# A down projection rearranged: 32 of its 44 feature tiles as seven block products with 512 moving columns

## The chip, the core and the metric

The kernel runs on one core of a Trainium2 chip. The metric is device time in microseconds of one execution. A core has TensorE (PE in the profile, its weight loads as PEld), VectorE (DVE), ScalarE (ACT), GpSimd (POOL) and SyncE (SP). Transfers are issued from SP's queue (hardware descriptors) and from POOL's queue (POOL writes the descriptors, so each issue shows as a busy POOL instruction).

## What is computed

One layer of an encoder for 512 tokens of 2048 features in float32: a norm, one projection to queries, keys and values, three kinds of attention, an output projection with a residual, then the part that matters here:

```python
h = rmsnorm(x, ffn_norm[l])
g = causal_dwconv(jnp.einsum('bsd,df->bsf', h, w_gate[l]), conv_w[l], conv_b[l])
u = jnp.einsum('bsd,df->bsf', h, w_up[l])
x = x + jnp.einsum('bsf,fd->bsd', jax.nn.silu(g) * u, w_down[l])
return rmsnorm(x, final_norm)
```

`w_down` is 5632 x 2048, so the last product takes 44 tiles of 128 gated features to 16 tiles of 128 outputs, for 512 tokens.

## The kernel before

Every product of float32 operands is made of three products of rounded parts: `split` (L57 to L59) writes the rounded high part on ScalarE (L58) and the rest on VectorE (L59), and `mm3` (L61 to L64) multiplies low by high, high by low and high by high into one PSUM bank. So each weight tile must pass ScalarE and VectorE before TensorE can use it. The pool of split weights, `wspl`, has three buffers of 1024 columns: a split can be made only when TensorE has finished with the part three places back.

The program has these stages, in order: attention with its projections (to about 710 us), the output projection (to 851 us), four gate and up tiles computed plainly and then 40 by `strassen` (to 1757 us), and the down projection with the last norm (to the end). TensorE's order is that of the code (`manual_schedule` on PE). The other engines' orders are set by the scheduler of the framework, which places an instruction by its estimated costs among what is ready.

`strassen(f)` computes gate and up of one feature tile as seven products of 256 tokens (Winograd's form). Its tiles come from two rings: `z`, into which POOL adds a second weight block while it loads (L804, an accumulating transfer), and five buffers `a` of pool `r4`. The gated tile is stored on POOL's queue into `a_dram` in the layout [128, 44, 512].

The down projection, `down` (after L920), takes the gated features in 11 chunks of 4 tiles. `gated(c)` loads one chunk from `a_dram` on SP's queue (`araw`) and splits it; `load_unit` loads 1 MB of weights for four output tiles into `wraw` (two buffers of 1 MB) and splits it in halves. Per output tile 12 matmuls run with the weights stationary and 512 tokens moving into one bank `dn`, and VectorE adds the bank to the residual `x2` (L938), which stays in SBUF for the whole stage in eight buffers of `big`. The residual is loaded on POOL's queue (L979) when TensorE has finished with the operands of the last gate tile. The last chunk is computed for 256 tokens at a time, so that the last norm of the first half runs beside the matmuls of the second.

Chunk by chunk this is 10 x 192 matmuls of 512 columns and 2 x 192 of 256 columns.

Of the kernel before, what the change touches and what calls it, by code (L numbers as in the profile page):

```python
# [15 lines left out]
P = 128  # L16
S = 512
# [6 lines left out]
NCH = NFT // CH  # L24
NEG = -3.0e38
# [16 lines left out]
def trunk(ctx, tc, xT, wqkv, wo, wo15, wgu, wd, par, lam4, rel, out):  # L42
# [14 lines left out]
    def split(hi, lo, src):  # L57
        act.copy(out=hi, in_=src)  # L58
        dve.tensor_tensor(out=lo, in0=src, in1=hi.bitcast(F32), op=ALU.subtract)  # L59
# [48 lines left out]
    a_dram = dram.tile([P, NFT, S], F32, name="a_dram")  # L108
# [123 lines left out]
    with ExitStack() as actx:  # L232
# [166 lines left out]
        def finish(o, summer, n, eps, gain, slot):  # L399

            sq = tmp.tile([P, S], F32, tag="t2", name="osq")
            act.activation(sq, o, AF.Square)
            sh = tmp.tile([P, S], F32R, tag="t2", name="osh")
            sl = tmp.tile([P, S], F32R, tag="t2", name="osl")
            split(sh, sl, sq)
            yield 7
            bank = att_bank("ossq")
            pe.matmul(bank, summer, sl, start=True, stop=False)
            pe.matmul(bank, summer, sh, start=False, stop=True)
            rs = rsqrt(None, bank, n, eps, tmp, "o")  # L410

            def last():
                split(y1[0][slot], y1[1][slot], o)

            dve.scalar_tensor_tensor(out=o, in0=o, scalar=gain, in1=rs, op0=ALU.mult, op1=ALU.mult)
            if slot >= KT - 2:
                pending.append(last)
            else:
                pool.dma_start(y_dram[:, slot, :], o)
# [277 lines left out]
    with ExitStack() as actx:  # L697
        fp = actx.enter_context(tc.tile_pool(name="fp", bufs=2))
        r4 = actx.enter_context(tc.tile_pool(name="r4", bufs=5))
# [24 lines left out]
        def new_g():  # L724
            g = fp.tile([P, 2 + 2 * S], F32, tag="g", name="g")
            pool.memset(g[:, 0:2], 0.0)
            return g, g[:, 2 + S : 2 + 2 * S]

        def plain(f):
# [12 lines left out]
            dve.tensor_tensor(out=u, in0=bu, in1=rs2, op=ALU.mult)  # L742
            dve.tensor_tensor(out=u, in0=u, in1=cv, op=ALU.mult)
            pool.dma_start(a_dram[:, f, :], u)
# [42 lines left out]
        def strassen(f, first=False):  # L787
# [18 lines left out]
            def later():  # L806
                a12, a22 = block("a12"), block("a22")
                sync.dma_start(a12, wgu[f, 0][:, half[1]])
                sync.dma_start(a22, wgu[f, 1][:, half[1]])
                return a12, a22  # L810

            def halves(src):
                wh = wspl.tile([P, 1024], F32R, tag="wh", name="wh")
                wl = wspl.tile([P, 1024], F32R, tag="wl", name="wl")
                split(wh, wl, src)
                return wh, wl
# [5 lines left out]
            lo, hi = slice(0, HS), slice(HS, S)  # L822
            U = fp.tile([P, HS], F32, tag="U", name="U", bufs=2)
# [26 lines left out]
            if first:  # L850
# [14 lines left out]
            else:  # L865
# [10 lines left out]
            w2 = halves(a12)  # L876
            add(a12, s2)
            product(w2, second, 1, bank1[:, lo], False, True)
            act.copy(out=g[:, 2 : 2 + HS], in_=bank1[:, lo])
            product(halves(a12), second, 2, bank2[:, lo], False, False)  # L880
            product(halves(a22), sums_, 3, bank2[:, hi], False, True)
            dve.tensor_tensor(
                out=g[:, 2 + HS : 2 + HS + S].rearrange("p (a b) -> p a b", b=HS),
                in0=bank2.rearrange("p (a b) -> p a b", b=HS),
                in1=U.unsqueeze(1).to_broadcast([P, 2, HS]),
                op=ALU.add,
            )
            cv, silu = convolved(f, g)
            dve.scalar_tensor_tensor(out=u, in0=u, scalar=-1.0, in1=cv, op0=ALU.mult, op1=ALU.mult)
            pool.dma_start(a_dram[:, f, :], u)  # L890
            return silu
# [6 lines left out]
        second = []  # L898
        for f in range(NPLAIN, NFT):
            silu = strassen(f, f == NPLAIN)  # L900


    with ExitStack() as actx:
        fp = actx.enter_context(tc.tile_pool(name="fp", bufs=2))
        x2 = None

        def gated(c):

            raw = wraw.tile([P, CH, S], F32, tag="raw", name="araw")
            sync.dma_start(raw, a_dram[:, c * CH : (c + 1) * CH, :])  # L910
            ah, al = [], []
            for i in range(CH // 2):
                j = (c % 2) * 2 + i
                h, l = [big.tile([P, 2, S], F32R, tag=f"b{x}{j}", name=f"a{x}") for x in "hl"]
# [5 lines left out]
        ssum3 = h2p.tile([P, S], F32, tag="ssum", name="ssum3")  # L920

        def down(units, a, t=slice(0, S), after=None, between=None):
            w = t.stop - t.start
            for g, halves in enumerate(units):
                for mm in range(4):
# [12 lines left out]
                    dve.tensor_tensor(out=x2[m][:, t], in0=bank, in1=x2[m][:, t], op=ALU.add)  # L938
                    if after is not None:
                        after(m, t)  # L940
                if between is not None:
                    next(between)

        def squares(m, t):
            sq = fp.tile([P, S], F32, tag="g", name="sq3")
# [6 lines left out]

        def last_norm(t, queues):
# [4 lines left out]
            rsqrt(rs3[:, t], ssq, D, NORM_EPS, fp, "n3", 3)  # L958
# [15 lines left out]
        a = gated(0)  # L974
        x2 = []
        for j in range(4, 8):
            for x in "hl":
                t = big.tile([P, 2, S], F32, tag=f"b{x}{j}", name="x2")
                pool.dma_start(t, x_dram[:, len(x2) : len(x2) + 2, :])  # L979
                x2 += [t[:, n, :] for n in range(2)]  # L980
# [5 lines left out]
        with tc.issue_after(silu):  # L986
            act.preload_act_table_set("natural_log_exp_and_others")
        t0, t1 = slice(0, S // 2), slice(S // 2, S)

        kept = [  # L990
            [h2p.tile([P, 1024], F32R, tag=f"h2{x}{i}", name=f"k{x}{i}") for x in "hl"] for i in range(8)
        ]
        kept = [kept[2 * g : 2 * g + 2] for g in range(4)]
        down((load_unit(wd[NCH - 1, g], kept[g]) for g in range(4)), a, t0, squares)
        down(kept, a, t1, squares, last_norm(t0, (sync,)))
# [71 lines left out]
```

## Time and profile before

| | |
|---|---|
| median of 3 runs | 2254.25 us (2253.73 to 2255.53) |
| the profiled execution, its own time | 2253.81 us |
| its span, first to last instruction | 2252.1 us |
| TensorE busy | 2209.6 us (98%), 14012 matmuls |
| VectorE busy | 1511.4 us (67%) |
| ScalarE busy | 992.8 us (44%) |
| POOL busy | 264.8 us (12%) |
| read from HBM, written to it | 305.65 MB, 27.79 MB |

How to read it: busy time is the union of an engine's instructions. A matmul's duration is its latency; matmuls overlap, and what one costs is the distance between the starts of two in a row. A group of instructions shows its line, engine, operation, the names of what it writes and reads, its shape and count, then its busy time, the mean duration of one, and the idle time of the engine just before. `SPq` and `POOLq` are the queues on which a transfer was issued; the number behind it is the median time from issue to landing.

### The profile page before, as it was taken

The page shows a single profiled execution, that of the slowest core. Times are in us where ns is not written, and L with a number is a line of the kernel's source. Part 1 is how long each engine was busy: PE and PEld are TensorE (multiplying, and loading weights), DVE is VectorE, ACT ScalarE, POOL GpSimd, SP SyncE. Part 2 cuts the span into 40 slices and gives each one's busy share as a digit, 9 for nine tenths or more (in the row PEclk, how much of TensorE's full clock was granted, in tenths as well). Part 3 has the DMA queues.
Part 4 walks back from the last instruction along what each step waited for, and adds up shares of the span by engine and source line. Part 5 has one row for each costly group of instructions (what it writes and reads, how often), then busy time and mean ns, then how long its engine had stood idle before and what let it go on. Part 6 is the DMA issues. An engine that isn't in the chain of part 4 may idle for free.

```text
span 2252.1 us, 34744 instructions
## 1 busy us (share of the span) xinstructions
PE 2209.6 (98%) x14012; PEld 2010.3 (89%) x14012; DVE 1511.4 (67%) x2169; ACT 992.8 (44%) x1482; POOL 264.8 (12%) x509
## 2 busy tenths in 40 slices
PE   8999999999999999999999999999999999999997
PEld 7888898788888888799999999999999888888887
DVE  6766667787677547777777777777777655555565
ACT  5555455566565323444444444444444322222232
POOL 0100001212112221011101111011110000000003
PEclk9999999999999999999999999999999999999999
DMA  5222222122234445867777777778775533333332
GB/s 196 99 80 85 99 80 90 64 87 72 97 126 158 169 137 205 272 182 204 193 197 186 204 200 198 190 189 206 198 196 154 210 113 112 131 118 125 131 131 76
DMA packets 79729, 335.69 MB, mean 149 GB/s; under 512 B 9424, under 2 KB 14288, under 8 KB 63184
## 3 DMA queue, kind: packets, MB, share of 16 engines
q1 hardware_dynamic: 56896, 257.32, 34.4%
q0 software_dynamic: 21376, 74.99, 14.4%
q8 instruction: 110, 1.80, 0.3%
q10 hardware_dynamic: 1296, 1.17, 0.2%
q14 instruction: 51, 0.42, 0.1%
HBM read 305.65 MB, written 27.79 MB: 148 GB/s over the span
## 4 chain that ended last, share of the span: by engine, by line
PE 90%; DVE 4%; ACT 2%; issue 1%; DMA 1%; POOL 1%; SPq 0%; POOLq 0%; DVEq 0%; ACTq 0%
PE c L64 36%; PE dn L64 21%; PE wo L64 8%; PE v L64 7%; PE q L64 6%; PE k L64 6%; PE tr L379 1%; PE g L64 1%; PE pv L64 1%; PE sc L349 1%; PE sc L348 1%; DVE l L530 1%; POOL z L500 1%; DVE wl L59 1%; PE u L64 0%
## 5 line engine op out<-in xcount | busy, mean ns | idle before, releaser
L58 ACT CAST wh<-raw 128x1024 fp32r<-128x1024 f32 (+1 forms) x227 | 236.1, 1041 | 502.1 <-PE dn L64 299.0
L59 DVE TENSOR_TENSOR wl<-a,wh 128x1024 fp32r<-128x1024 f32 x199 | 243.5, 1224 | 190.3 <-ACT wh L58 190.2
L64 PE MATMUL c<-bl,wh 128*128 128x256 f32 x1280 | 363.4, 284 | 3.8 <-ACT wh L58 3.8
L64 PE MATMUL c<-bh,wl 128*128 128x256 f32 x1280 | 363.3, 284 | 1.5 <-DVE wl L59 1.5
L64 PE MATMUL c<-bh,wh 128*128 128x256 f32 x1280 | 363.2, 284 | 0.0
L59 DVE TENSOR_TENSOR wl<-raw,wh 128x1024 fp32r<-128x1024 f32 (+1 forms) x227 | 274.4, 1210 | 96.3 <-ACT wh L58 95.7
L58 ACT CAST wh<-a 128x1024 fp32r<-128x1024 f32 x199 | 208.8, 1049 | 242.8 <-DVE a L819 205.0
L64 PE MATMUL c<-h2l,wh 128*128 128x256 f32 x960 | 271.8, 283 | 0.9 <-DVE U L844 0.9
L64 PE MATMUL c<-h2h,wh 128*128 128x256 f32 x960 | 271.7, 283 | 0.0
L64 PE MATMUL c<-h2h,wl 128*128 128x256 f32 x960 | 271.7, 283 | 0.0
L64 PEld LDWEIGHTS c<-bl,wh 128*128 128x128 f32 x1280 | 246.8, 193 | 4.0 <-ACT wh L58 4.0
L64 PE MATMUL dn<-al,wh 128*128 128x512 f32 x640 | 249.2, 389 | 0.7 <-DVE al L59 0.7
L938 DVE TENSOR_TENSOR x<-dn,x 128x512 f32<-128x512 f32 (+1 forms) x192 | 124.0, 646 | 187.1 <-PE dn L64 183.6
L64 PE MATMUL dn<-ah,wl 128*128 128x512 f32 x640 | 249.0, 389 | 0.0
L64 PE MATMUL dn<-ah,wh 128*128 128x512 f32 x640 | 249.0, 389 | 0.0
L64 PEld LDWEIGHTS c<-bh,wl 128*128 128x128 f32 x1280 | 246.7, 193 | 1.8 <-DVE wl L59 1.8
L64 PEld LDWEIGHTS c<-bh,wh 128*128 128x128 f32 x1280 | 246.7, 193 | 0.0
L64 PEld LDWEIGHTS c<-h2l,wh 128*128 128x128 f32 x960 | 184.3, 192 | 1.1 <-DVE U L844 1.1
L64 PEld LDWEIGHTS c<-h2h,wl 128*128 128x128 f32 x960 | 184.3, 192 | 0.0
L64 PEld LDWEIGHTS c<-h2h,wh 128*128 128x128 f32 x960 | 184.3, 192 | 0.0
L64 PE MATMUL v<-wl,hh 128*128 128x256 f32 x512 | 147.9, 289 | 10.1 <-DVE wl L59 9.2
L64 PE MATMUL v<-wh,hl 128*128 128x256 f32 x512 | 145.8, 285 | 0.4 <-DVE hl L161 0.4
(242 smaller groups left out, 4690.9 us busy)
## 6 DMA issues: line engine op xcount, KB each, us to landing
a<-in_wgu SPq DMA_DIRECT2D x121, 512.0 KB, 4.7
raw<-in_wqkv SPq DMA_DIRECT2D x46, 1024.0 KB, 4.8
raw<-in_wd SPq DMA_DIRECT2D x44, 1024.0 KB, 4.8
z<-in_wgu SPq DMA_DIRECT2D x80, 512.0 KB, 5.7
z<-in_wgu POOLq DMA_DIRECT2D x78, 512.0 KB, 9.8
raw<-in_wo SPq DMA_DIRECT2D x16, 1024.0 KB, 4.8
a_dram<-g POOLq DMA_DIRECT2D x44, 256.0 KB, 6.0
araw<-a_dram SPq DMA_DIRECT2D x11, 1024.0 KB, 4.9
```

The lines of the kernel that those rows point to most:

```text
L58: act.copy(out=hi, in_=src)
L59: dve.tensor_tensor(out=lo, in0=src, in1=hi.bitcast(F32), op=ALU.subtract)
L64: pe.matmul(o, l[x], r[y], start=start and i == 0, stop=stop and i == 2, skip_group_check=on)
L348: pe.matmul(bank[:, kt], q[c][:, qt], k[c][:, kt], start=True, stop=False)
L349: pe.matmul(bank[:, kt], q[c][:, qt], kh[c][:, kt], start=False, stop=True)
L379: pe.transpose(out=bank[:, (i - j) * P : (i - j + 1) * P], in_=w[:, o : o + P], identity=ident)
L500: pool.affine_select(out=t[:, o : o + P], in_=t[:, o : o + P], pattern=[[-1, P]], compare_op=ALU.is_gt, fill=fill, base=0, channel_multipl ...
L530: dve.tensor_tensor_scan(back, back, back, 0.0, ALU.add, ALU.max)
L938: dve.tensor_tensor(out=x2[m][:, t], in0=bank, in1=x2[m][:, t], op=ALU.add)
```

## The change

Chunks 0 to 7 (feature tiles 0 to 31) are no longer computed by `down`. They are computed four chunks at a time as a two by two block product, seven products instead of eight, with the gated features stationary and 512 columns of weights moving. The outputs are then tokens by features, are stored, and at the end are turned on TensorE and added to the residual. Chunks 8 to 10 stay in `down`. In parts:

- **Stores.** `store` puts tiles 0 to 31 into `ab_dram`, by halves of 256 tokens. For tiles 4 to 7, 12 to 15, 20 to 23 and 28 to 31, `tile_before` loads the tile stored four places earlier (two loads of 128 KB on SP), and `token_sums` makes the four sums of token halves on VectorE (four 128x256 operations) and stores them in `t_dram` (two stores of 256 KB on POOL). It writes into `g` and `cv`, which the tile has finished with.
- **Weights' sums for the first unit.** Beside attention, POOL copies four weight units of 1 MB from DRAM to DRAM (after the outputs of heads 0 to 3) and adds others to them by accumulating transfers (after heads 4 to 7).
- **The last gate tile** (`last=True`) runs its products in another order, those on `second` first, with separate banks, so that the buffers of `second` come free four products before its end.
- **`Seven`.** Four units: two groups of four chunks, times two pairs of 512 output columns. A unit has 28 steps (seven products, two blocks, two halves). A step splits 1024 columns of weights (L1127 on ScalarE, L1129 on VectorE) and issues 12 matmuls of 512 columns (two feature slices, two token tiles, three each). VectorE forms the weights' sums in place (`prepare`, `prepare_6`; the first unit finds half of its sums formed). The weights go through four buffers of 1 MB (`wraw` and a new pool `rw`). The gated operands, 14 per group of chunks, are loaded on POOL's queue through two buffers `fe` (the first four into freed buffers) and split by the table FIRST or NEXT at given steps. `sums` adds the products up out of PSUM and stores them on POOL into `c_dram`. This part has its orders on all engines from the code.
- **`turned`.** After a group of matmuls of chunks 8 and 9, two 1 MB tiles of `c_dram` are loaded on SP, added on VectorE (128x2048), turned by 16 transposes into four banks, and added to or taken from `x2`.
- The residual is loaded during the last unit; the load of ScalarE's tables moves from the end of the down projection to its beginning.

Counted over the program: 1536 matmuls of `dn` with 512 columns go; 1344 of the same shape into the seven products' banks `r`, and 64 transposes of 128x128, come.

```diff
+NSEV = 32
+    ab_dram = dram.tile([P, 2, NSEV, S // 2], F32, name="ab_dram")
+    t_dram = dram.tile([P, 4, NSEV // 2, S // 2], F32, name="t_dram")
+    a_dram = dram.tile([P, NFT - NSEV, S], F32, name="a_dram")
+    s_dram = [dram.tile([P, 2048], F32, name=f"s_dram{i}") for i in range(4)]
+    c_dram = [dram.tile([P, NB, D], F32, name=f"c_dram{i}") for i in range(NSEV // 16)]
...
+                if slot < 8:
+                    i = slot % 4
+                    b, w = divmod(i, 2)
+                    with tc.issue_after(stored):
+                        if slot < 4:
+                            pool.dma_start(s_dram[i], wd[2 * b, 0] if w else wd[2 * b + 1, 1])
+                        else:
+                            pool.dma_start(s_dram[i], wd[2 * b, 1], accum_op=ALU.add, max_dma_last_dim=8192)
...
+            dve.tensor_tensor(out=t1, in0=b11, in1=b12, op=ALU.subtract)
+            dve.tensor_tensor(out=t3, in0=b22, in1=b12, op=ALU.subtract)
+            for dst, x, y in ((t2, b22, t1), (t4, t2, b21)):
+                dve.scalar_tensor_tensor(out=dst, in0=x, scalar=-1.0, in1=y, op0=ALU.mult, op1=ALU.subtract)
+            for n, t in ((0, t12), (2, t34)):
+                pool.dma_start(t_dram[:, n : n + 2, f // 8 * 4 + f % 4, :], t.rearrange("p (a b) -> p a b", b=HS))
...
+            def parts(self, between):
+                src = self.src
+                wh = wspl.tile([P, 1024], F32R, tag="wh", name="wh")
+                wl = wspl.tile([P, 1024], F32R, tag="wl", name="wl")
+                hv, lv = [w.rearrange("p (i m c) -> p m i c", i=2, m=4) for w in (wh, wl)]
+                act.copy(out=hv, in_=src)
+                between()
+                dve.tensor_tensor(out=lv, in0=src, in1=hv.bitcast(F32), op=ALU.subtract)
+                self.ws = wh, wl
+            def multiply(self, k):
...
+                for i in range(2):
+                    o, w = (2 * h + i) * HS, slice(i * S, (i + 1) * S)
+                    for t in range(2):
+                        q = slice(o + t * P, o + (t + 1) * P)
+                        mm3(self.banks[r][t], (f[0][:, q], f[1][:, q]), (self.ws[0][:, w], self.ws[1][:, w]),
...
+            def sums(self, k):
...
+                elif k == 26:
+                    e = self.out_tile()
+                    for t in range(2):
+                        act.copy(out=e[:, t, :], in_=r["1"][t])
+                    self.put(e, 0, 0)
+                elif k == 28:
+                    e = self.out_tile()
+                    for t in range(2):
+                        add(e[:, t, :], r["5"][t], self.U[:, t, :])
+                    self.put(e, 0, 1)
...
+                for mm in range(4):
+                    x = x2[4 * g + mm]
+                    bank = acc_bank("ct")
+                    for t in range(NB):
+                        pe.transpose(
+                            out=bank[:, t * P : (t + 1) * P], in_=cs[0][:, t, mm * P : (mm + 1) * P], identity=ident
+                        )
+                    dve.tensor_tensor(out=x, in0=x, in1=bank, op=ALU.subtract if g % 2 else ALU.add)
...
-        a = gated(0)
...
-        for c in range(NCH - 1):
-            down((load_unit(wd[c, g]) for g in range(4)), a)
-            a = gated(c + 1)
+        rest = turned()
+        a = gated(c0, 14)
+        for c in range(c0, NCH - 1):
+            down((load_unit(wd[c, g]) for g in range(4)), a, plus, between=rest)
+            a = gated(c + 1, 8 if c == c0 else 14)
```

Two places in the order of instructions are spoken of below. The first is VectorE in the reduction. Before, in a chunk of `down` (`x2` the residual, `dn` a bank, `wl` and `al` the low parts of weights and features):

```order
L938 TENSOR_TENSOR x2_18096<-dn_18224,x2_18096 128x512
L59 TENSOR_TENSOR wl_18307<-raw_18304,wh_18306 128x1024
L938 TENSOR_TENSOR x2_18098<-dn_18248,x2_18098 128x512
L59 TENSOR_TENSOR al_18373<-araw_18370,ah_18372 128x1024
L59 TENSOR_TENSOR al_18377<-araw_18370,ah_18376 128x1024
L938 TENSOR_TENSOR x2_18098<-dn_18262,x2_18098 128x512
```

Now, at the opening of the second unit (`c`, `U` sums out of the banks `r5`, `r7`; `raw<-raw` and `sh`, `sl` the sums of weights):

```order
L1068 TENSOR_TENSOR c_18870<-r5_18323,U_18537 128x512
L1068 TENSOR_TENSOR c_18870<-r5_18324,U_18537 128x512
L1068 TENSOR_TENSOR raw_18823<-raw_18821,raw_18823 128x4x256
L1129 TENSOR_TENSOR wl_18875<-raw_18819,wh_18874 128x4x2x128
L1068 TENSOR_TENSOR raw_18823<-raw_18821,raw_18823 128x4x256
L1129 TENSOR_TENSOR wl_18892<-raw_18823,wh_18891 128x4x2x128
L1068 TENSOR_TENSOR U_18537<-r7_18365,U_18537 128x512
L1068 TENSOR_TENSOR U_18537<-r7_18366,U_18537 128x512
L1068 TENSOR_TENSOR raw_18821<-raw_18821,raw_18819 128x4x256
L1129 TENSOR_TENSOR wl_18914<-raw_18823,wh_18913 128x4x2x128
L1068 TENSOR_TENSOR sh_18918<-raw_18823,raw_18819 128x1024
L1068 TENSOR_TENSOR raw_18821<-raw_18821,raw_18819 128x4x256
```

Between two splits of weights there now stand sums of weights and sums out of PSUM, where before one or two residual additions stood. The second place is POOL's queue where the last gate tile meets the reduction. Before:

```order
L890 DMA a_dram_82<-g_17618 128x512
L979 DMA x2_18092<-x_dram_81 128x1024
L979 DMA x2_18090<-x_dram_81 128x1024
L979 DMA x2_18094<-x_dram_81 128x1024
L979 DMA x2_18096<-x_dram_81 128x1024
L979 DMA x2_18098<-x_dram_81 128x1024
L890 DMA a_dram_82<-g_17846 128x512
```

Now (`fh`, `fl` and `f` are the first gated operands):

```order
L752 DMA a_dram_84<-g_17765 128x512
L1047 DMA fh_18238<-ab_dram_82 128x1024
L1051 DMA fl_18239<-t_dram_83 128x1024
L1051 DMA fh_18240<-t_dram_83 128x1024
L1051 DMA fl_18241<-t_dram_83 128x1024
L1047 DMA f_18252<-ab_dram_82 128x1024
L1051 DMA f_18254<-t_dram_83 128x1024
L752 DMA a_dram_84<-g_17993 128x512
```

The residual's eight loads have gone from here to the last unit, and six loads of gated operands, 512 KB each, stand in their place.

More of the change, by code (lines that the diff above doesn't have):

```diff
@@ L918, in gated, with down @@
             return ah, al
-        ssum3 = h2p.tile([P, S], F32, tag="ssum", name="ssum3")
-        def down(units, a, t=slice(0, S), after=None, between=None):
+        def down(units, a, add, t=slice(0, S), between=None):
             w = t.stop - t.start
@@ L937, in down @@
                         )
-                    dve.tensor_tensor(out=x2[m][:, t], in0=bank, in1=x2[m][:, t], op=ALU.add)
-                    if after is not None:
-                        after(m, t)
+                    add(m, t, bank)
                 if between is not None:
-                    next(between)
-        def squares(m, t):
-            sq = fp.tile([P, S], F32, tag="g", name="sq3")
+                    next(between, None)
+        ORDER = [(n, b) for b in range(2) for n in (1, 5, 7, 6)] + [(n, b) for b in range(2) for n in (2, 3, 4)]
@@ new lines, in feature_parts, with weights, add @@
+        def feature_parts(i, src):
+            p = pair(10 + i if i < 6 else i - 6, name="f")
+            split(*p, src)
+            return p
+        raws = [0]
+        def weights(src):
+            raws[0] += 1
+            raw = (rw, wraw)[raws[0] % 2].tile([P, 2048], F32, tag="raw", name="raw")
+            sync.dma_start(raw, src)
+            return [raw.rearrange("p (m i c) -> p m i c", m=4, i=4)[:, :, 2 * h : 2 * h + 2, :] for h in range(2)]
+        def add(dst, x, y):
+            dve.tensor_tensor(out=dst, in0=x, in1=y, op=ALU.add)
```

311 lines of the change are left out of this document (263 added, 48 removed).

## The prediction

> **What bounds the kernel now.** I read the page first: busy shares, the granted clock by slices, the chain.
>
> ```profile
> span 2252.1 us, 34744 instructions
> PE 2209.6 (98%) x14012; PEld 2010.3 (89%) x14012; DVE 1511.4 (67%) x2169; ACT 992.8 (44%) x1482; POOL 264.8 (12%) x509
> ...
> PEclk9999999999999999999999999999999999999999
> ...
> PE 90%; DVE 4%; ACT 2%; issue 1%; DMA 1%; POOL 1%; SPq 0%; POOLq 0%; DVEq 0%; ACTq 0%
> ```
>
> TensorE is busy nearly all the time at full clock and carries 90% of the chain. Next I read the chain in order of time, for the stages that the change touches.
>
> ```profile
> 959.16 792.27 PE c L64 x6600
> 1756.68 462.93 PE dn L64 x2154
> 2220.05 15.84 PE dn L64 x132
> ```
>
> From 959 us to 2236 us the chain is matmuls alone: first gate and up (`c`), then the down projection (`dn`), with no other engine between. What an instruction of TensorE less is worth there is its full distance to the next one. Third, the busy time by stretches, and TensorE's waits from 951 us to 2220 us.
>
> ```profile
> core 0: us, PE busy (x) PEld busy (x) DVE busy (x) ACT busy (x) POOL busy (x), PEclk, DMA share, GB/s
> ...
> 959.00:1757.00 798.00, 797.10 (x6631) 796.28 (x6632) 582.13 (x634) 365.90 (x436) 95.12 (x157) 1.00 0.73 191
> 1757.00:2220.00 463.00, 463.00 (x2157) 388.33 (x2156) 247.42 (x291) 120.01 (x127) 14.67 (x21) 1.00 0.36 129
> 2220.00:2252.10 32.10, 18.01 (x147) 17.40 (x145) 22.73 (x53) 7.80 (x19) 8.47 (x12) 0.84 0.40 132
> ```
> ```profile
> engine line waited for: us in total, times, longest us
> PE c L64 <- DVE U L844: 0.9, 1, 0.9
> PE dn L64 <- DVE al L59: 0.7, 1, 0.7
> ```
>
> In the down projection TensorE has work at every moment, while VectorE is busy 247 of 463 us and the transfers fill 36%. There is room beside TensorE, and that is where the change puts its additions; whether they fit is the question.
>
> **What goes and comes on TensorE.** The price of a matmul of 512 columns is read where nothing else runs, in the stretch of `dn` alone; that of a transpose from the timeline of TensorE in attention, where five stand in a row.
>
> ```profile
> 1800.00:2000.00 200.00, 200.00 (x884) 165.61 (x883) 50.47 (x73) 1.00 0.33 116
> ```
> ```profile
> 400.06 0.71 PE L379 MATMUL tr<-ident,z 128*128 128x128 f32 x5
> ```
> ```profile
> L64 PE MATMUL dn<-al,wh 128*128 128x512 f32 x640 | 249.2, 389 | 0.7 <-DVE al L59 0.7
> ...
> L379 PE MATMUL tr<-ident,w 128*128 128x128 f32 x160 | 27.9, 272 | 0.0
> ```
>
> 884 matmuls in 200 us are 0.2262 us each; the 389 ns of a group's mean is latency, of which 163 ns overlap. 1536 of them go and 1344 of the same shape and type come: 192 x 0.2262 = 43.4 us less. Five transposes in 0.71 us, the last with its latency of 0.27, start (0.71 - 0.27) / 4 = 0.11 us apart: 64 of them cost 7.0 us more. Net on TensorE: -36.4 us. That the new matmuls hold a feature slice and stream weights changes neither shape nor type, so I leave their price; if it differed by 1 ns, it would be 1.3 us.
>
> The Trainium skill (TensorE: Matmul & The Clock Gate, Part 4: PE-mode transpose) gives about 275 ns for a 128x128 transpose in a kernel's context, and speaks so far against the change: 64 would be 17.6 us and the net -25.8 us. This case's row has the same 272 ns, but as latency; the starts lie 0.11 us apart, and the row decides.
>
> **Step time and its feeding.** A step of a unit is 12 matmuls, 12 x 0.2262 = 2.71 us; a unit of 28 steps is 76.0 us. Beside it VectorE has to do far more than `down` asked of it. Its prices:
>
> ```profile
> L59 DVE TENSOR_TENSOR wl<-raw,wh 128x1024 fp32r<-128x1024 f32 x223 | 272.7, 1224 | 95.4 <-ACT wh L58 94.9
> ...
> L938 DVE TENSOR_TENSOR x<-dn,x 128x512 f32<-128x512 f32 x160 | 110.6, 691 | 169.0 <-PE dn L64 165.6 <-DMA x<-x_dram 3.5
> ...
> L819 DVE TENSOR_TENSOR a<-a,z 128x1024 f32<-128x1024 f32 x40 | 49.0, 1225 | 1.4
> ...
> L844 DVE TENSOR_TENSOR U<-c,U 128x256 f32<-128x256 f32 x40 | 17.0, 425 | 13.8 <-ACT U L843 13.8
> ```
>
> In the second unit: 28 splits, 16 sums of weights and 7 splits of features, 51 x 1.225 = 62.5 us, and ten sums out of PSUM, 6.9 us: 69.4 of 76.0 us. The first unit has 8 sums fewer and 6 features more (67 us), the third equals the second, the fourth has no features (61 us). So VectorE fits on average, at 91% in the worst, but not evenly: what counts is how far a split may come late. ScalarE, 1.05 us per split, has 43 us and fits.
>
> ```profile
> 1403.02 1.05 ACT L58 CAST wh<-a 128x1024 fp32r<-128x1024 f32 x1 [0.81 <-PE c L64]
> ```
> ```profile
> 1404.18 1.22 DVE L59 TENSOR_TENSOR wl<-a,wh 128x1024 fp32r<-128x1024 f32 x1
> ```
>
> From the moment TensorE frees a buffer to the end of the split into it are 2.4 us (1403.02 to 1405.40). With three buffers the split is wanted two steps, 5.4 us, after that: a lead of 3.0 us. The worst place is the opening of each unit after the first, whose order stands above: from the sums out of `r5` to the split of the sixth step VectorE has 11 operations of 1.225 and four of 0.69 us, 16.2 us, against five steps of 13.6 us. The 2.6 us too much eat the lead of 3.0. The sums there also wait: those of `c` for the store of the previous `c` (one buffer), whose price is bounded by the nearest rows of POOL's queue:
>
> ```profile
> a<-in_wgu SPq DMA_DIRECT2D x121, 512.0 KB, 4.7
> raw<-in_wd SPq DMA_DIRECT2D x44, 1024.0 KB, 4.8
> ...
> z<-in_wgu POOLq DMA_DIRECT2D x78, 512.0 KB, 9.8
> ...
> b_dram<-b POOLq DMA_DIRECT2D x8, 512.0 KB, 4.6
> x<-x_dram POOLq DMA_DIRECT2D x8, 512.0 KB, 9.9
> xin<-in_xT SPq DMA_DIRECT2D x7, 512.0 KB, 10.1
> ```
>
> ScalarE fills that `c` after step 23; with 2.4 us of ScalarE and 4.6 us for a plain 512 KB store it has landed 7.5 us after that step's end, about when VectorE arrives (two steps and 2.4 us, 7.8 us). With 9.8 us, an accumulating load's, it would hold VectorE, with all splits queued behind, some 4 us in each unit: 16 us. I take 1 us per opening and 2 us for step 17 and the feature splits of the first unit, 5 us; bounds 0 and 16.
>
> **Entering the units.** POOL's first feature load waits for the last product on `second`, four products of 24 matmuls (24 x 792.27 / 6600 = 2.9 us) before the end, 11.5 us. Four loads of 512 KB then run at once with three of 1 MB on SP, which wait for the last split into `r4`'s ring, about 6 us before the end. At the 218 GB/s of the `raw<-in_wd` row the first features land after 5 us and are split before the end; the second weight unit, wanted 5.4 us after it, lands about 2 us after the end and still has two splits to pass, behind the tail of the last gate tile (two convolution steps, four sums, a product) on VectorE. I take 3 us; bounds 0 and 8 (if the loads come one after the other). The old entry cost 0.7 us.
>
> **Leaving them, and the turn.** The chunks' first splits stand ahead of the last sums, so chunk 8 starts with its weights ready. Each of the four turned groups needs its second `c_dram` tile loaded (4.8 us) after the transposes before it freed the buffer, and added in 2.3 us (1.225 and twice the step from 0.69 to 1.225): 7.1 us in the 10.9 us of 48 matmuls. Cover 3.8 us. I take 2 us for both; bounds 0 and 8. The 16 additions of banks to `x2`, 0.69 each, lie under matmuls.
>
> **The parts beside other stages.** `token_sums` puts 4 x 0.425 = 1.7 us on VectorE into 16 gate tiles, at this place:
>
> ```profile
> 1415.62 1.23 DVE L59 TENSOR_TENSOR wl<-z,wh 128x1024 fp32r<-128x1024 f32 x1 [0.20 <-ACT wh L58]
> 1416.77 0.69 DVE L889 SCALAR_TENSOR_TENSOR g<-g,cv 128x512 f32<-128x512 f32 x1
> 1417.78 0.42 DVE L844 TENSOR_TENSOR U<-c,U 128x256 f32<-128x256 f32 x1 [0.33 <-ACT U L843]
> 1418.73 1.23 DVE L59 TENSOR_TENSOR wl<-a,wh 128x1024 fp32r<-128x1024 f32 x1 [0.52 <-ACT wh L58]
> ```
>
> 1.05 us of it are idle time there; the other 0.65 us eat into the lead. I take 0; without that cover 16 x 0.65 = 10 us. Its two stores stand ahead of the next `z` accumulation on POOL, whose operand is wanted a whole tile (20 us) later. In attention POOL issues eight transfers of 1 MB. What is queued behind them there is the negated maximum of a softmax, for which ScalarE waits:
>
> ```profile
> L804 POOL DMA_DIRECT2D z<-in_wgu x78 | 68.9, 1033 | 33.2 <-ACT wh L58 16.4 <-DMA z<-in_wgu 7.0 <-issue 5.5
> L369 POOL TENSOR_SCALAR mx<-mx 128x1 f32<-128x1 f32 x96 | 31.7, 331 | 219.4 <-DVE mx L359 200.3 <-DVE r L436 6.8 <-ACT vv L290 5.4
> ```
>
> An accumulating issue of half the bytes keeps POOL 1.03 us, so at most about 2.1 us, eight times, hidden while TensorE has projections between: 0, with 8 us kept as the far end.
>
> **The sum.** -36.4 + 5 + 3 + 2 = -26.4 us. Against the profiled execution's 2253.81 us that is 2227.4; the median of the runs is 0.44 above it: 2227.9 us. With no wait at all it is 2217.9.
>
> **Rivals.** *VectorE sets the pace.* The new operations read and write views of four dimensions in runs of 128 elements, which no row here shows. For it: 91% leaves little. If each of the 51 cost 20% more, 1.47 us, a unit would need 81.9 of 76.0 us: three units at 6 us and the fourth about even, 18 us more with the openings' waits no longer covered, some 8: 2254 us less 36.4, plus 10 and 26, is 2254; half of that surcharge gives 2241. Against it: operations with 128x1024 cost 1.22 whatever their operands. I take 2241 for this case.
>
> *Late transfers, slower than before.* A unit moves 10 MB of weights, 3.5 of features and 2 of outputs in 76 us, 204 GB/s, as much as the gate stage at a 73% share. The shortest notices are those of the second block's two sums operands and of the next unit's, four to five steps (11 to 14 us). At the pace of the start-up (512 KB in 10.1 us) a 1 MB load takes 20 us, 8 us too long, twice a unit: 64 us, so 2254.25 - 36.4 + 64 = 2282 us. It decides against the change from about 4.6 us lost at each of these eight places. Against it: 1 MB takes 4.8 us in the median today, and a late load delays one place, as the queue catches up.
> The Trainium skill (TensorE: Matmul & The Clock Gate, What's actually happening) adds that an idle TensorE falls to half clock after some 3.4 us and needs as long to return: up to 1.7 us for each such wait, 14 us for eight. The last row of the stretches (0.84, where TensorE idles 14 of 32 us) agrees.
>
> *It does what it says, and the gain is eaten.* Attention and the gate stage pay their far ends (8 and 10 us) and the entry and turn theirs (16): 2254.25 - 36.4 + 8 + 10 + 16 + 5 is 2257, no change.
>
> **Chances.** Forecast (2216 to 2236) 0.75; VectorE's pace (2236 to 2250) 0.15; eaten (2250 to 2259) 0.04; late transfers 0.06. A difference of 0.2%, 4.5 us, is about what a measurement of this kernel can tell from none. Faster by more: 0.75 + 0.15 = 0.90; same 0.04; slower 0.06. The range takes in the forecast and half of the second case: 2216 to 2243.
>
> **What would show it.** In the profile after: 1344 matmuls `r` starting 0.226 us apart and a stage of 305 to 313 us; TensorE's waits there mostly for `wl`, at the first steps of a unit and step 18, each under 1.5 us; transposes in 0.11 us; a chain still of TensorE from 959 us on. I am wrong if `wl` or `sh` operations last over 1.3 us, if TensorE waits in attention for more than before, or if ScalarE's idle time is ended by `raw` or `f` loads.

## The result, and the profile after

The changed kernel takes 2220.22 us (median of 4 runs, 2218.57 to 2223.95) against 2253.99 us before: a ratio of 0.9853 with a 95% interval of 0.9836 to 0.987, 33.8 us less. Forecast were 2227.9 us, with a range of 2216 to 2243. The profiled execution is the slowest of the four, 2223.95 us with a span of 2222.2 us. First the page of the changed kernel: the span, the busy shares, and the chain by engines.

```profile
span 2222.2 us, 34979 instructions
...
PE 2176.9 (98%) x13884; PEld 1984.2 (89%) x13884; DVE 1614.7 (73%) x2283; ACT 1060.1 (48%) x1558; POOL 324.1 (15%) x593
...
PE 87%; DVE 5%; DMA 3%; ACT 2%; issue 2%; POOL 1%; SPq 0%; POOLq 0%; DVEq 0%; ACTq 0%
```

TensorE is as busy as before, with 128 matmuls fewer (192 less, 64 transposes more), and VectorE has 103 us more to do. DMA now stands in the chain with 3%; where, the chain in order of time shows.

```profile
1741.77 11.80 PE c L66 x96
...
1765.13 4.64 DMA f<-ab_dram
...
1775.85 7.48 DMA f<-t_dram
...
1792.78 8.61 DMA f<-t_dram
...
1810.96 256.14 PE r L66 x1128
2067.10 21.76 PE dn L66 x96
2088.87 1.75 PE ct L1268 x16
2090.61 10.90 PE dn L66 x48
2101.52 1.75 PE ct L1268 x16
```

From 1811 us to the end of the fourth unit the products run without any other engine in the chain, then `dn` and the transposes `ct`, with nothing between them. Only in the first unit, from 1765 to 1811 us, does the chain go through loads of features (`f`). The busy time by stretches (the gate stage, the four units, the chunks with the turn) and TensorE's waits say the same:

```profile
core 0: us, PE busy (x) PEld busy (x) DVE busy (x) ACT busy (x) POOL busy (x), PEclk, DMA share, GB/s
941.20:1759.10 817.90, 809.57 (x6721) 808.67 (x6720) 612.77 (x711) 373.94 (x445) 124.28 (x191) 0.99 0.77 212
1759.10:1838.30 79.20, 76.92 (x338) 62.84 (x338) 63.65 (x62) 43.87 (x46) 9.10 (x16) 1.00 0.69 247
1838.30:1914.50 76.20, 76.20 (x338) 63.13 (x337) 65.18 (x62) 38.00 (x39) 6.72 (x11) 1.00 0.61 214
1914.50:1990.80 76.30, 76.30 (x338) 63.01 (x337) 65.05 (x62) 38.10 (x39) 5.64 (x9) 1.00 0.57 200
1990.80:2067.00 76.20, 76.20 (x338) 63.12 (x337) 59.46 (x57) 33.22 (x34) 7.14 (x12) 1.00 0.62 228
2067.00:2190.00 123.00, 123.00 (x690) 107.73 (x689) 79.83 (x101) 34.62 (x45) 12.56 (x18) 1.00 0.47 167
```
```profile
PE c L66 <- ACT wh L59: 4.7, 1, 4.7
PE r L66 <- DVE wl L1129: 2.3, 2, 1.9
```

Units two to four take 76.2 us each, 0.2268 us for each of their 336 matmuls, and TensorE never waits in them. The first takes 79.2: two waits for `wl`. The `wl` named there is only the last link. VectorE and then POOL before the second of these waits:

```profile
1799.28 1.22 DVE L1129 TENSOR_TENSOR wl<-raw,wh 128x1024 fp32r<-128x1024 f32 x1 [1.45 <-ACT wh L1127]
1802.49 1.23 DVE L60 TENSOR_TENSOR fl<-f,fh 128x1024 fp32r<-128x1024 f32 x1 [1.99 <-ACT fh L59]
1803.63 1.22 DVE L1068 TENSOR_TENSOR sh<-sh,raw 128x1024 f32<-128x1024 f32 x1
1804.77 1.22 DVE L1129 TENSOR_TENSOR wl<-raw,wh 128x1024 fp32r<-128x1024 f32 x1
...
1808.55 1.22 DVE L1068 TENSOR_TENSOR sl<-sl,raw 128x1024 f32<-128x1024 f32 x1
```
```profile
1765.13 0.53 POOL L1047 DMA_DIRECT2D f<-ab_dram  x1 [17.39 <-DVE g L970]
...
1792.78 0.53 POOL L1051 DMA_DIRECT2D f<-t_dram  x1 [6.29 <-DVE fl L60]
```

At 1801 us VectorE stood idle for 2 us, since the features to be split had not landed (8.6 us after their issue at 1792.78). All that is queued behind, the split for step 18 among it, then runs back to back and comes 2 us late. The load had been issued so late because POOL waited for one of only two buffers `f` (6.29 us, until a split had read it). The first wait, 0.4 us, has a late load as its root too: the buffers `f` lie in memory of the gate stage, and their first load waits for the product of the last gate tile (17.39 us, `g`).

Where the 29.9 us between the two profiled spans came from, by the starts of matmuls: from the last `c` to the last `dn` 483.0 us before (1754.02 to 2237.03) and 448.5 after (1759.03 to 2207.49), 34.6 us less; the norm behind them 0.3 less; attention with its output projection ended 2.6 us later (the last matmul of `wo`, here and below) and the gate stage took 2.5 us more. The last two are of the single execution, as the experiments show. Beside the median's 33.8 us the 34.6 is the change.

### The profile page after: what moved, and what is told of

Same layout as the page of the kernel before. It is cut to its first block, busy times and chain, and to the rows that moved or that the text cites. A ratio compares the mean times of both kernels' runs of the same rounds, so it can differ in the third digit from the quotient of the medians.

```text
span 2222.2 us, 34979 instructions
## 1 busy us (share of the span) xinstructions
PE 2176.9 (98%) x13884; PEld 1984.2 (89%) x13884; DVE 1614.7 (73%) x2283; ACT 1060.1 (48%) x1558; POOL 324.1 (15%) x593
## 4 chain that ended last, share of the span: by engine, by line
PE 87%; DVE 5%; DMA 3%; ACT 2%; issue 2%; POOL 1%; SPq 0%; POOLq 0%; DVEq 0%; ACTq 0%
PE c L66 36%; PE r L66 12%; PE wo L66 8%; PE v L66 8%; PE q L66 6%; PE k L66 6%; PE dn L66 6%; PE tr L388 1%; DMA f<-t_dram 1%; PE pv L66 1%; PE sc L358 1%; PE sc L357 1%; DVE l L548 1%; POOL z L518 1%; DMA xt<-x_dram 1%
## 5 line engine op out<-in xcount | busy, mean ns | idle before, releaser
L59 ACT CAST wh<-raw 128x1024 fp32r<-128x1024 f32 (+1 forms) x163 | 168.6, 1035 | 257.4 <-PE wo L66 85.1
L60 DVE TENSOR_TENSOR wl<-raw,wh 128x1024 fp32r<-128x1024 f32 (+1 forms) x163 | 197.6, 1214 | 65.6 <-ACT wh L59 64.9
L66 PE MATMUL r<-wl,fh 128*128 128x512 f32 x448 | 174.8, 390 | 2.3 <-DVE wl L1129 2.3
L66 PE MATMUL r<-wh,fh 128*128 128x512 f32 x448 | 174.4, 389 | 0.0
L66 PE MATMUL r<-wh,fl 128*128 128x512 f32 x448 | 174.3, 389 | 0.0
L66 PE MATMUL v<-wh,hh 128*128 128x256 f32 x512 | 147.0, 287 | 0.0
```

What stands on the lines that cost most here:

```text
L59: a = act.copy(out=hi, in_=src)
L60: d = dve.tensor_tensor(out=lo, in0=src, in1=hi.bitcast(F32), op=ALU.subtract)
L66: pe.matmul(o, l[x], r[y], start=start and i == 0, stop=stop and i == 2, skip_group_check=on)
```

## The experiments

All are compared with runs of the kernel before on the same chip. There were three chips, on which the kernel before took 2253.61 us (the control, feature loads, sums of tokens and attention's transfers), 2255.13 (16 tiles first, idle tile, fourteen operations, loads twice) and 2254.42 (the others). Where a time is set against the control's, up to 1.5 us of the difference can be the chip's.

**The changed kernel once more.**

> The changed kernel once more, unaltered. Both theories: 0.985 of the time before, about 2220 us. Theory (the stage of the seven products pays only for late feature loads): again two stalls of TensorE in the first unit, about 0.6 and 2.0 us, none in the other three units. Attention, which was 2.6 us longer in the profile after than in the profile before, ends anywhere within 3 us of 850 us if that is chance; if the eight transfers cost it, it is again 2 to 3 us late.

2220.69 us, ratio 0.9853 (0.984 to 0.9867). TensorE's waits in the units, in its profile:

```profile
PE r L66 <- DVE wl L1129: 1.6, 1, 1.6
```

One wait this time, the larger; two were expected. Attention ended at 851.8 us. In the profiles of the twelve runs that keep attention's transfers, the changed kernel's first one included, it ended between 849.3 and 853.0, on average at 851.2; before at 850.5. From the first to the last `c` it was 813.6 us here, 817.8 in the first profile after and 815.4 before: at the first tile of `strassen` TensorE waits for `wh` 4.7 us in one execution and 2.7 in the other. So neither the 2.6 nor the 2.5 us is a cost of the change. Over the twelve profiles attention ended 0.7 us later and the gate stage took 0.9 us more (816.3) than in the one profile before; a cost of that size is not excluded.

**Feature loads earlier.**

```python
early = {0: 8, 2: 9, 4: 7, 6: 6, 10: 7}   # feature: pair of buffers that lies idle
if not c and i in early:
    staged[:] = pair(early[i], F32, "f")
src = staged.pop(0) if staged else fe.tile(...)
...
for _ in range(6):                          # before: 2
    load_features()
...
if at[s] > (0, 13) or at[s][1] in (4, 5, 8, 9, 12, 13):   # before: at[s] > (0, 3)
    load_features()
```

> The first unit's feature loads 4 to 13 are issued earlier, into buffers that lie idle there, so that each has landed long before its split. Theory (late feature loads): both stalls of the first unit go, 2.6 us less than the changed kernel, about 2217.6 us, and 1344 products take 304 to 305 us. Rival (VectorE's operations at steps 17 and 18 are too many, as the prediction had it): the stall before step 18 stays at about 2 us, and the time at 2220 us.

2217.52 us, ratio 0.9839 (0.9825 to 0.9852). The chain of this kernel in order of time:

```profile
1752.97 2.76 PE c L66 x23
1755.73 304.95 PE r L66 x1344
2060.68 21.76 PE dn L66 x96
```

All 1344 products stand in a row in 305 us, with no wait. VectorE executes the same operations in the same order as in the changed kernel (only the buffers that the features land in differ), so the late loads were the cause, and not VectorE's amount of work at steps 17 and 18. This is the fastest version of the study. The intervals of its ratio and the control's overlap; that it saves 2 us and more rests on the trace, where the first unit takes 76.4 us instead of 78.4 and 79.2.

**No sums of tokens in the gate stage** (the call of `token_sums` and the loads of `tile_before` left out, the products then read other features).

> Left out: the sums of tokens in 16 gate tiles, with their two loads and two stores each (the products then take other features in the place of these sums). Theory (hidden beside TensorE): the gate stage stays at 818 us within 1 us, and the time at 2220 us within 2. Rival (each such tile loses 0.65 us of VectorE's lead): 10 us less, 2210 us.

2220.97 us, ratio 0.9855 (0.9841 to 0.9868): nothing. From the first to the last `c` 816.2 us, inside the spread above. The 64 small operations, 32 loads and 32 stores are wholly hidden.

**No transfers in attention**: the first unit loads the weights themselves and forms its sums.

```python
if slot < 8:                      ->  if False:
self.formed = c == g == 0         ->  self.formed = False
```

> Without the eight transfers of 1 MB in attention: the first unit forms its eight sums of weights itself, as the others do. Theory (the transfers cost attention nothing; VectorE has room in the first unit: 61.5 us busy and 8 x 1.14 more of 76.3): 2220 us within 2, no new stall over 1 us in the unit. Rivals: the transfers cost attention 2.6 us (2217.5) up to 8 us (2212); or the first unit has no room, and some 3 us or more are lost there (2223 and above).

2229.8 us, ratio 0.9901 (0.9887 to 0.9914): 9 us slower than the changed kernel. Attention ended at 850.2 us, within the spread of the others. The loss is in the first unit, which took 91.6 us, some 13 more than in the changed kernel. The whole lost less than the unit: against the control's profile, attention ended 1.7 us earlier here and the gate stage took 0.5 us less, which chance does as well. TensorE's waits there, and two rows of VectorE at its entry and soon after:

```profile
PE r L66 <- DVE wl L1129: 9.7, 8, 2.6
```
```profile
1754.04 1.23 DVE L1068 TENSOR_TENSOR raw<-raw 128x1024 f32<-128x1024 f32 x1 [0.59 <-DMA raw<-in_wd]
...
1763.73 1.22 DVE L1068 TENSOR_TENSOR sh<-raw 128x1024 f32<-128x1024 f32 x1
```

From 1754 to 1774 us VectorE works without a gap, and every split comes late. My theory, that 70.6 us fit into 76.3, was wrong: the average does not decide it. The rival held: the first unit has no room at its entry. So the eight transfers cost attention nothing that these runs can tell (1 to 2 us would not show), and are worth 9 us in all.

**Eight operations more in the first unit, in two ways.** First the additions that the unit was spared, written to an idle tile:

> The changed kernel with eight additions of 128x1024 more on VectorE in the first unit, where the other units form their sums of weights (here the results go to an idle tile); weights, transfers and attention are as in the changed kernel. Theory (the first unit is short of VectorE at its entry, though it is busy only 61 of 77 us on average): most of the 13 us that the kernel without attention's transfers lost in this unit come back, 10 to 13 us, 2231 to 2233 us. Rival (those 13 us came from the loads of the weights, or VectorE fits by its average): within 3 us of 2220.

2238.24 us, ratio 0.9926 (0.9911 to 0.9941), more than either expectation. One wait of TensorE of 10.1 us at the entry was the experiment's own: the idle tile lies in memory that the store of the last gated tile still read, and all of VectorE's work stood behind it:

```profile
PE r L66 <- DVE wl L1134: 16.1, 7, 10.1
```
```profile
1766.11 1.23 DVE L1068 TENSOR_TENSOR spare<-raw 128x1024 f32<-128x1024 f32 x1 [7.11 <-DMA a_dram<-g]
```

So the operations were added where they need no tile, by doing the split's subtraction twice in eight steps:

```python
if steps[0] in (3, 4, 5, 6, 11, 12, 13, 14):
    dve.tensor_tensor(out=lv, in0=src, in1=hv.bitcast(F32), op=ALU.subtract)
```

> Eight more operations of VectorE in the first unit (its half of the split is done twice in steps 3 to 6 and 11 to 14), without the idle tile for which the earlier run waited. Theory (the first unit has no room for eight operations in these places, whatever its average; in the kernel without attention's transfers it waited 9.7 us for `wl`, 2.6 of them at its first step): 7 to 11 us more than the changed kernel, 2227 to 2231 us. Rival (63 us busy and 9.1 more are under the unit's 76.2, so they fit): within 3 us of 2220.

2227.81 us, ratio 0.9882 (0.9867 to 0.9897), 7.1 us above the control; the unit took 86.0 us. Its waits:

```profile
PE r L66 <- DVE wl L1133: 7.3, 7, 1.9
```

Eight operations of 1.14 us, 9.1 us, cost 7 to 8 us in this unit, although VectorE is busy 73.1 of its 86.0 us. The rest of the 13 us without attention's transfers was not taken apart by a run. Its trace shows what the run with eight operations lacks: the weights to be added land as VectorE gets there (0.59 us of idle time above), TensorE waits 2.6 us at the unit's second step, and the granted clock is 0.82 from 1751.5 to 1761 us and 0.95 from 1811 us to the unit's end.

**Fourteen, and seven, operations more in each of units two to four** (the same doubled subtraction, in every second step and in every fourth).

> The changed kernel with VectorE's half of the split done twice in every second step of units two to four, 14 operations of 128x1024 more in each. Theory (such operations start 1.137 us apart when they stand in a row, not 1.225: 65, 66 and 61 us of 76.3 busy): 15.9 us more each are 4.6, 5.3 and 1 us too much, 11 us in all and at most 3 for the openings: 2231 to 2234 us. Rival (1.225 each, as the prediction had it: 69.4, 69.4 and 61 us): 10.2, 10.2 and 1.9 us too much and the openings, 22 us and more, 2242 us or above.

2239.61 us, ratio 0.9933 (0.9916 to 0.995), 18.9 us above the control, and between the two expectations. The busy time in its three units:

```profile
1834.40:1916.80 82.40, 78.73 (x337) 62.45 (x336) 81.12 (x76) 37.66 (x39) 6.72 (x11) 1.00 0.53 193
1916.80:2001.30 84.50, 78.67 (x337) 62.44 (x336) 81.80 (x76) 37.75 (x39) 5.64 (x9) 1.00 0.52 185
2001.30:2081.80 80.50, 77.97 (x337) 62.60 (x336) 75.88 (x71) 33.21 (x34) 7.13 (x12) 1.00 0.58 216
```

The price was nearer the theory's than the rival's: 15.9 to 16.8 us of busy time more in each, 1.14 to 1.20 for an operation. The loss was larger than the average gives: the units are 1.3, 2.7 and 4.6 us longer than VectorE's own work, and the fourth, whose work would have fitted (75.9 of 76.2), lost 4.3 us.

> As the run with 14 more operations of VectorE in units two to four, with seven in each. Measured there: units of 82.4, 84.5 and 80.5 us with VectorE busy 81.4, 81.6 and 75.7, so the fourth lost 4.3 us though its average fitted. Theory (what counts is where the operations stand; a lead of about 3 us covers seven of them but for the openings): 73, 73 and 67 us busy, 0 to 4 us lost in all, 2220 to 2224 us. Rival (each operation costs at the same rate as there, 18.8 us for 42): 9.4 us, 2230 us.

2224.14 us, ratio 0.9866 (0.9852 to 0.9881), 3.5 us above the control. The interval overlaps the control's; that time is lost rests on the trace. The units took 77.5, 79.3 and 76.8 us with VectorE busy 73.3, 73.4 and 67.6: 4.9 us lost, just above the theory's 4, half of the rival's 9.4. So VectorE's pace begins to show where it is busy for 88 to 96% of 76.2 us (67.6 and 73.4), by where the operations stand, and the changed kernel's 86% lies just below.

**Sixteen tiles instead of 32** (`NSEV = 16`).

> Seven products for 16 of the 44 feature tiles instead of 32: two units, one table of outputs. Theory (the gain is TensorE's count: a unit takes 48 matmuls of 0.2262 us away, 10.9 us, the transposes cost 7.0 us once, the first unit 2.6 us of stalls once): 2 x 10.9 - 7.0 - 2.6 = 12.1 us less than before, 2241.7 us. Rival (no costs that come once; the gain goes with the number of tiles): half of the 33.8 us, 2236.8 us.

2252.55 us, ratio 0.9991 (0.9981 to 1.0): no gain, against both expectations. The waits of its `dn`:

```profile
PE dn L66 <- DVE al L60: 6.1, 5, 1.9
```

The new wait is the edit's: after the change the chunks take turns at two sets of buffers only once, which is enough for three chunks and not for seven. With the turns for all of them:

```python
a = gated(c + 1, 8 if c == c0 else 14)  ->  a = gated(c + 1, 14 if (c - c0) % 2 else 8)
```

> Sixteen feature tiles in seven products as in the earlier run, but the seven chunks of four tiles that stay with `down` take turns at two sets of buffers, which that run did only once. Theory (that run lost some 9 us at five chunk boundaries to this; the gain is TensorE's count): 2 x 10.9 - 7.0 - 2.5 = 12.3 us less than before, 2242 us, and no wait of `dn` over 0.5 us. Rival (half the units bring nothing): 2252 us again.

2244.03 us, ratio 0.9952 (0.9937 to 0.9967), 10.4 us less than its runs of the kernel before; expected were 12.3. No wait of `dn` is left. The first unit lost 4.7 us instead of 2.5: its two waits were as in the changed kernel (2.3 us), but a stretch at lower clock followed (below). So the gain is 10.9 us for each unit, less 7.0 for the turn and what the first unit loses, both only once: 32 tiles bring some three times what 16 bring.

**Weights loaded twice** (units two to four, the same load issued twice into the buffer).

> Every load of weights of units two to four is done twice into the same buffer, so that what took 6 us lands some 5 us later and these units move 20 instead of 10 MB of weights. Theory (the notice of four to five steps, 11 to 14 us, is enough): 2220 us, at most 3 more. Rival (late transfers, as in the prediction: it decides from 4.6 us lost at each of two places a unit): 6 places of 2 to 5 us, 2232 to 2250 us.

2276.56 us, ratio 1.0099 (1.0081 to 1.0117): slower than the kernel before, and above both expectations. My step of 5 us was wrong, since the second load waits on SP for the landing of the first. Rows of SP's queue, then SP's waits, VectorE's and TensorE's:

```profile
1848.22 0.33 SPq L1065 DMA_DIRECT2D raw<-in_wd  x1
1853.07 0.33 SPq L1066 DMA_DIRECT2D raw<-in_wd  x1
1853.49 0.38 SPq L1065 DMA_DIRECT2D raw<-in_wd  x1
1860.36 0.33 SPq L1066 DMA_DIRECT2D raw<-in_wd  x1
```
```profile
SPq L1066 <- DMA raw<-in_wd: 183.6, 28, 11.0
```
```profile
DVE raw L1070 <- DMA raw<-in_wd: 53.4, 6, 11.8
```
```profile
PE r L66 <- DVE wl L1131: 41.7, 7, 9.6
```

The six waits of VectorE are of two kinds. Three are at the sums of a unit's second block, 11.3, 10.0 and 8.7 us. The two operands of such a sum are issued 1.1 us apart in the changed kernel; here the repeat of the second starts 12 us after the first load (1848.22 to 1860.36) and lands 19.4 us after it, instead of 8.0. A delay of 11.4 us that costs 11.3 was not covered. The landings in the first profile after confirm it: at these three places (units two to four) the second operand lands 1.0, 0.1 and 0.1 us before VectorE reads it, while from the second unit on every other load has 3 us or more. The other three waits are at the openings of the units, 1.3, 11.8 and 10.2 us, though the changed kernel has 7 to 8 us to spare there: every repeat also holds up the loads behind it on SP, so these come later still.

In the three units TensorE lost 54 us: 40.0 in five waits, 10 in 51 matmuls that started 0.43 us apart, and the rest in smaller pieces. So the rival of late transfers was nearer than I had it, and the second block's loads would decide it first. Its price was not too high: 8 us a place in the prediction, some 11 at each of five here.

**The last gate tile in its old order.**

```python
silu, u_last = strassen(NFT - 1, last=True)  ->  strassen(NFT - 1)   # old order, u kept for the store
```

> The last gate tile in the old order of its products, so that the operands `second` are used up to the last but one product instead of up to the fifth last. Theory (the new order is what hides the entry: the first feature loads start when `second` comes free, 11.5 us before the products end; with the old order 2.9 us): the first product of the first unit starts 6 to 9 us late, 2226 to 2230 us. Rival (the entry is hidden by other work): within 2 us of 2220.

2231.24 us, ratio 0.9895 (0.9879 to 0.9912), 10.5 us above the control. TensorE's waits at the entry, and ScalarE's:

```profile
PE r L66 <- ACT fh L59: 8.1, 1, 8.1
PE r L66 <- DVE fl L60: 1.9, 1, 1.9
```
```profile
1758.21 1.04 ACT L59 CAST fh<-fl 128x1024 fp32r<-128x1024 f32 x1 [8.38 <-DMA fl<-t_dram]
```

The first features are not there, the first product starts 8.3 us late, its second matmul waits again, and half clock follows. The 6 to 9 us expected for the late start hold; the time is 1.2 us above the range expected, which left out the second wait and the stretch at lower clock. The new order hides the entry.

## Why the prediction was right, and which terms were not

The sum had the right mechanism and the right main term; the reserves for stalls were too large. Forecast were 26.4 us less, measured 33.8 (median) and 34.6 (from the last `c` to the last `dn` in the profiles). With the terms as measured the sum is -43.5 + 7.0 + 2.6 + 0.1 = -33.8 us.

- **What goes and comes on TensorE** (-43.4 + 7.0). Right. A unit without waits is 0.2268 us a matmul, so 192 are 43.5 us, and the transposes are four times 1.75 us, 0.109 us each: 7.0 us. The Trainium skill (TensorE: Matmul & The Clock Gate, Part 4: PE-mode transpose) with its 275 ns for bf16 would have made them 17.6 us, as an estimate; the trace has that as the duration of one (272 ns) and not as its cost in a row of them.
- **Step time and its feeding** (5 us; measured 2.6, the mean of 79.2 and 78.4 us for the first unit less 76.2, and another cause). Two steps failed. First "51 x 1.225 = 62.5 us, and ten sums out of PSUM, 6.9 us: 69.4 of 76.0 us": VectorE was busy 65.2 us. The rows above show why: operations of 1.22 us start 1.14 us apart when they stand in a row (1803.63, 1804.77), so the mean duration of a group overstates a full queue by 7%. With 1.14, and 0.66 for sums out of PSUM (four of them start between 1805.90 and 1808.55 there), an opening needs 15.2 instead of 16.2 us, and the lead of 3.0 us covers it: no opening waited. Second, the 2 us at "step 17 and the feature splits of the first unit" came at that place, but from late loads, as the run with earlier loads showed. That the sums of `c` wait for the store of the previous `c` happened once, 2.0 us on VectorE, and TensorE did not notice:

```profile
L1068 DVE TENSOR_TENSOR c<-r,U 128x512 f32<-128x512 f32 x16 | 10.7, 688 | 2.3 <-DMA c_dram<-c 2.0
```

- **Entering** (3 us; measured 0.1). The term "I take 3 us" was too large, the mechanism right. POOL issued the first feature load 13.5 us before the first product; the second weight unit was issued 6.1 us before it and landed after 6.3:

```profile
1745.62 0.54 POOL L1047 DMA_DIRECT2D fh<-ab_dram  x1
```
```profile
1753.05 0.85 SPq L1064 DMA_DIRECT2D raw<-s_dram  x2
```

VectorE finished its split at 1762.4 us, and it was wanted at 1764.6, two steps after the start at 1759.15. The tail of the gate tile, which I put ahead of it, was spread between the splits.

- **Leaving, and the turn** (2 us; measured 0). The cover of 3.8 us held: the chain goes from `dn` to `ct` and back without a piece between. VectorE waited for a load of `cs` once, 1.6 us, under `dn`.
- **The parts beside other stages** (0 and 0). Right as far as single executions differ, by the runs without them: no change without the token sums, none that can be told from chance in attention without its transfers.
- **The rivals.** VectorE did not set the pace: with views of four dimensions `wl` lasts 1.22 us and `sh` 1.22, as before, so the surcharge that was its condition is not there. But seven operations more per unit already cost 4.9 us in three units. Late transfers did not decide either; the loads that I named as the shortest, the second block's sums operands, were indeed the ones, with a spare of 0.1 to 1.0 us and not the several microseconds that four to five steps against 4.8 us seem to leave. Both terms were off: the notice of the second operand is 7 to 8 us and not 11 to 14 (in the second unit it is issued at 1850.28 and read at 1858.18), and it takes 6.8 to 7.9 us, as it goes out with two others (landing after 4.8, 6.9 and 9.0 us in that unit). That the late loads cost nothing in these units was luck and no working of the prediction.
- **The signs.** The stage of 305 to 313 us came (307.8). The waits were fewer than foretold, none at the opening of a later unit; the longest, 1.9 and 1.6 us at step 18 (counted from 0), were above the 1.5 us given. And one sign of being wrong did come: ScalarE's idle time was ended by loads of `f`, which is the second failed step above.

```profile
L59 ACT CAST fh<-f 128x1024 fp32r<-128x1024 f32 x24 | 25.2, 1050 | 10.6 <-DMA f<-t_dram 6.9 <-DMA f<-ab_dram 3.7
```

## What to carry to other kernels

For an engine whose queue is full, price its work by the distance between starts in a row, not by the mean duration of a group: here 1.14 against 1.22 us, the difference between a queue with 86% and one with 91%. When a wait names the engine that feeds TensorE, go one link further back before blaming its amount of work: here an idle gap of 2 us in that engine, ended by a load, was the cause, and buffers that lay idle removed it. And look at the least spare time of a load rather than at the mean share of the transfers: transfers that were busy 57% and 62% of the third and fourth units stood beside loads that landed 0.1 us before their use.

## What the runs showed of the hardware

A wait of TensorE can cost more than its length, and how much depends on the execution. In the run with 16 tiles and the mended buffers, a wait of 1.92 us was followed, 1.5 us later, by eight matmuls 0.43 us apart instead of 0.23:

```profile
1808.45 0.50 PE L66 MATMUL r<-wl,fh 128*128 128x512 f32 x1 [1.92 <-DVE wl L1129]
...
1809.96 0.63 PE L66 MATMUL r<-wl,fh 128*128 128x512 f32 x1
1810.39 0.63 PE L66 MATMUL r<-wh,fl 128*128 128x512 f32 x1
```

The granted clock from 1809 to 1814 us was 0.66. The same wait at the same step in the changed kernel, 1.9 us long, was followed by nothing of the kind. The Trainium skill (TensorE: Matmul & The Clock Gate, What's actually happening) tells of a window of 3.4 us that runs free of the kernel, and of half clock after one that was idle. The chance in these rows agrees with a free-running window, but 1.92 us of idle time are less than a whole one: here less than the page's window was enough. After the 8.1 and 1.9 us of waits at the entry with the last gate tile in its old order the clock was 0.52 from 1763 to 1771 us. Whether this is also why attention ended anywhere from 849.3 to 853.0 us in kernels that are the same there was not tested.
